# First-stage stores issued by ScalarE, split tiles doubled, rotation tables single

## The chip, the cores and the metric

The kernel runs on one core of one Trainium2 chip. The time is that of one execution on the device, in microseconds (us). TensorE (PE in the profile) multiplies, VectorE (DVE), ScalarE (ACT) and GpSimd (POOL) do elementwise work, and SyncE (SP) issues nearly all transfers. A transfer that SyncE, ScalarE or GpSimd issues runs on the core's 16 DMA engines. An engine takes its instructions in the order in which they stand in its queue, a transfer that it issues among them.

## The reference, cut to what matters

Two token groups (256 prompt tokens, 2048 noisy latent tokens) pass through two layers with the same weights. A layer normalises and modulates its input, projects it to 15 column groups, runs four mixers side by side and projects back:

```python
h = (rms_norm(x) * (1.0 + scale) + shift)
(da_q, da_k, da_v, da_g, s5_u, s5_g, hg_q, hg_ff, hg_fb, hg_i, hg_g,
 mla_cq, mla_ckv, mla_kr, mla_g) = split_columns(h @ P["w_in"][l])
q_r = rope_2d(q, *pos); k_all = concat([rope_2d(k, *pos), ck])   # differential attention
kr_lat = rope_2d(kr, *pos)                                       # latent attention
x = x + gate * (concat([a_out, b_out, c_out, d_out]) @ P["w_out"][l])
```

The outputs also hold the prompt's keys, values and final states of each layer. All is float32.

## The kernel before

A layer is run in three phases: `first_stage`, `mixers`, `out_proj`. Matmuls that need float32 accuracy are made of three: each operand is split by `split2` into a high part (a cast to fp32r, line 169, here on ScalarE) and a low part (the difference, line 173, here on VectorE), and `mm3` (lines 177 to 179) multiplies high by high, high by low and low by high.

`first_stage` weaves two generators. The one is `proj1`, in six blocks of 384 tokens. `prep` normalises the next block (`h_block`: transposing matmuls `pst` of line 299, scale and shift by ScalarE on line 304, high part `hhi` and low part `hlo` by VectorE) and `keep` stores both parts, 1.5 MB each, to `HD` (line 440). A block then has five column groups in the order dak0, dak1, daq0, daq1, cqk (keys, queries, and the rotated part of the latent keys with half of the compressed query): 24 matmuls each into a `psF` tile, followed by `evac1`; then three tiles `psT` of 24 matmuls, copied to `evT` (line 499) and stored to `VT` (line 500).

`evac1` is a chain through two engines. ScalarE copies the result from PSUM to `x32` (line 372 or 364, one buffer), VectorE turns it in four instructions with the tables `cos` and `sin` (`rope`, lines 324 to 328, one buffer), ScalarE casts the high part to `sphi` or `krhi` (one buffer under one tag), VectorE makes the low part `splo` or `krlo` (likewise), and SyncE stores: three transfers for keys and queries (`store_qk`, line 355), two for the rotated latent key (`store_kr`, lines 349 and 350). The buffer of a tile is free again when its last transfer has landed. In the last block, which holds the prompt, `out_tr` also transposes pieces of `x32` with matmuls `pso` (line 338) and stores them. `cache_keys` sends 256 cached keys down the same path at the start.

The other generator, `s5_build`, makes the tables of the state-space mixer: GpSimd and VectorE work out 16 groups (`wz`, `so`, `cp`, `Eb`), TensorE transposes and multiplies small tiles (`pswz`, `psk`, lines 1302 and 1307), ScalarE copies the results to `so` and `mp`, SyncE stores `SC` and `ED`.

PSUM in this stage: four buffers for `psF` and `psT` together (tag S), two for `pst` and `pso`, one each for two tags that `pswz` and `psk` share. A planner with a cost model orders the instructions of each engine when the program is built; the order is then fixed. The tables `cos` and `sin` come once per block by two transfers (`rope_tables`), and lie in a pool with two buffers. `rope_tables` and `out_tr` are also used in the next phase, there from a pool that has one buffer anyway.

Of the kernel before, what the change touches and what calls it, by code (L numbers as in the profile page):

```python
# [10 lines left out]
F32 = mybir.dt.float32  # L11
F32R = mybir.dt.float32r
# [12 lines left out]
LS = 2048  # L25
# [284 lines left out]
def rope_tables(g, p, tok0, n):  # L310
    nc = g.nc
    g.tab0 = tok0
    g.cos = p.tile([128, n], F32, tag="cos", name="cos")
    g.sin = p.tile([128, n], F32, tag="sin", name="sin")
    nc.sync.dma_start(g.cos, g.A["rcos"][:, tok0:tok0 + n])
    nc.sync.dma_start(g.sin, g.A["rsin"][:, tok0:tok0 + n])

# [14 lines left out]
def out_tr(g, p, src, rows, n, dst):  # L332
    nc = g.nc
    a, b = rows
    w = b - a
    for t in range(n // 128):
        ps = pst(g, "mm", "pso")
        nc.tensor.matmul(ps[:, :w], lhsT=src[a:b, t * 128:(t + 1) * 128], rhs=g.ident[a:b, a:b], start=True, stop=True)
        o = p.tile([128, 128], F32, tag="otr", name="otr")
        nc.scalar.copy(o[:, :w], ps[:, :w])  # L340
        nc.sync.dma_start(dst(t), o[:, :w])


def store_kr(g, p, src, tok0, n):
    nc = g.nc
    hi = p.tile([128, 384], F32R, tag="sphi", name="krhi", bufs=1)[64:96, :n]
    lo = p.tile([128, 384], F32R, tag="splo", name="krlo", bufs=1)[64:96, :n]
    split2(g, hi, lo, src)
    nc.sync.dma_start(g.KRD[0, 0:32, tok0:tok0 + n], hi.bitcast(F32))
    nc.sync.dma_start(g.KRD[1, 0:32, tok0:tok0 + n], lo.bitcast(F32))  # L350


def store_qk(g, dst, parts, idx, hi, lo, sl):
    for r, part in enumerate(parts):
        g.nc.sync.dma_start(dst[4 * idx:4 * idx + 4, r * 32:(r + 1) * 32, sl], (hi, lo)[part].bitcast(F32))


def evac1(g, l, p, kind, idx, ps, tok0, n):
    nc = g.nc
    sl = slice(tok0, tok0 + n)  # L360
    cut = min(max(LS - tok0, 0), n)
    x32 = p.tile([128, 384], F32, tag="x32", name="x32", bufs=1)
    if kind == "cqk":
        nc.scalar.copy(x32[:96], ps[:96, :n])
        r0 = FROW[(kind, idx)]
        nc.sync.dma_start(g.PF[r0:r0 + 64, sl], x32[:64])
        if cut < n:
            out_tr(g, p, x32[:, cut:], (64, 96), n - cut, lambda t: g.O["new_mla_krope"][l, t * 128:(t + 1) * 128, :])
        r32 = rope(g, p, x32, (64, 96), tok0, n, "rp")
        store_kr(g, p, r32[64:96], tok0, n)  # L370
        return
    nc.scalar.mul(x32, ps[:, :n], 32 ** -0.5 if kind == "daq" else 1.0)
    if kind == "dak" and cut < n:
        out_tr(g, p, x32[:, cut:], (0, 128), n - cut, lambda t: g.O["new_diff_k"][l, t * 128:(t + 1) * 128, idx * 128:(idx + 1) * 128])
    r32 = rope(g, p, x32, (0, 128), tok0, n, "rp")
    hi = p.tile([128, 384], F32R, tag="sphi", name="sphi", bufs=1)
    lo = p.tile([128, 384], F32R, tag="splo", name="splo", bufs=1)
    split2(g, hi, lo, r32)
    store_qk(g, g.QD if kind == "daq" else g.KD, (0, 0, 1) if kind == "daq" else (0, 1, 0), idx, hi, lo, sl)

# [25 lines left out]
def cache_keys(g, l, p):  # L406
    nc = g.nc
    for i in range(2):
        kc32 = p.tile([128, 384], F32, tag="x32", name="kc32", bufs=1)
        nc.sync.dma_start(kc32[:, :256], g.A["cdk"][l, i])  # L410
        hi = p.tile([128, 384], F32R, tag="sphi", name="sphi", bufs=1)
        lo = p.tile([128, 384], F32R, tag="splo", name="splo", bufs=1)
        split2(g, hi[:, :256], lo[:, :256], kc32[:, :256])
        store_qk(g, g.KD, (0, 1, 0), i, hi[:, :256], lo[:, :256], slice(NT, NK))
    kr32 = p.tile([128, 384], F32, tag="x32", name="kr32", bufs=1)[64:96, :256]
    nc.sync.dma_start(kr32, g.A["cmr"][l])
    store_kr(g, p, kr32, NT, 256)


def proj1(g, l):  # L420
    nc = g.nc
    N = 384
    with ExitStack() as es:
        px = es.enter_context(pool(g, "pjx", 2))
        ph0 = es.enter_context(pool(g, "pjh0", 1))
        pw0 = es.enter_context(pool(g, "pjw0", 1))
        pws = es.enter_context(pool(g, "pjs", 2))
        starts = list(range(0, NT, N))
        hs = {}

        def prep(i):
            ph = ph1 if i % 2 else ph0
            hi = ph.tile([128, 8, N], F32R, tag="hhi", name="hhi")
            lo = ph.tile([128, 8, N], F32R, tag="hlo", name="hlo")
            h_block(g, l, starts[i], N, px, hi, lo, mod if i == 0 else None)
            hs[i] = (hi, lo)

        def keep(i):
            for part, x in enumerate(hs[i]):
                nc.sync.dma_start(g.HD[part, :, :, starts[i]:starts[i] + N], x.bitcast(F32))  # L440

        mod = startup(g) if l == 0 else None
        pw = es.enter_context(pool(g, "pjw", 1))
        prep(0)
        ph1 = es.enter_context(pool(g, "pjh1", 1))
        p = es.enter_context(pool(g, "pj", 2))
        wf = []

        def load_f(k):
            m = len(FB1[k][2])  # L450
            w32 = pws.tile([128, 8, 128], F32, tag="w32", name="w32")
            q = pw0 if k == 0 else pw
            hi = q.tile([128, 8, 128], F32R, name=f"wfh{k}")
            lo = q.tile([128, 8, 128], F32R, name=f"wfl{k}")
            nc.sync.dma_start(w32[:, :, :m], g.A["wF"][l, k] if m == 128 else g.A["wFp"][l])
            split2(g, hi[:, :, :m], lo[:, :, :m], w32[:, :, :m], "act", "vec" if k == 0 else W1LO)
            wf.append((hi, lo))

        load_f(0)
        if l == 0:  # L460
            late_consts(g)
        for k in range(1, len(FB1)):
            load_f(k)
        wth = pw.tile([128, 8, 512], F32R, name="wth")
        wtl = pw.tile([128, 8, 512], F32R, name="wtl")
        for kc in range(0, 8, 2):
            w32 = pws.tile([128, 2, 512], F32, tag="w32", name="wt32")
            nc.sync.dma_start(w32, g.A["wT"][l, :, kc:kc + 2, :])
            split2(g, wth[:, kc:kc + 2, :], wtl[:, kc:kc + 2, :], w32, "act", W1LO)
        keep(0)  # L470
        yield
        cache_keys(g, l, p)
        for i, tok0 in enumerate(starts):
            if 0 < i < len(starts) - 1:
                prep(i + 1)
                keep(i + 1)
            if i == 2 and l == 0:
                for rows in [g.KRD[0, 32:34]] + [g.KD[i, 96:98] for i in range(8)]:
                    nc.sync.dma_start(rows.rearrange("o (a b) -> (o a) b", b=128), g.ones[0:2 * NK // 128, :])
            hi, lo = hs.pop(i)  # L480
            rope_tables(g, p, tok0, N)
            for k, (kind, idx, cols) in enumerate(FB1):
                if i == 0 and k == H1:
                    prep(1)
                    keep(1)
                m = len(cols)
                ps = pst(g, "mm", "psF")
                for kc in range(8):
                    mm3(nc, ps[:m, :N], wf[k][0][:, kc, :m], wf[k][1][:, kc, :m], hi[:, kc, :], lo[:, kc, :], kc == 0, kc == 7)
                evac1(g, l, p, kind, idx, ps, tok0, N)  # L490
                yield
            for t in range(N // 128):
                ts_ = slice(t * 128, (t + 1) * 128)
                tok = tok0 + t * 128
                ps = pst(g, "mm", "psT")
                for kc in range(8):
                    mm3(nc, ps, hi[:, kc, ts_], lo[:, kc, ts_], wth[:, kc, :], wtl[:, kc, :], kc == 0, kc == 7)
                o = p.tile([128, 512], F32, tag="ev", name="evT")
                nc.scalar.copy(o, ps)
                (nc.gpsimd if i + 1 == len(starts) else nc.sync).dma_start(g.VT[tok:tok + 128, :], o)  # L500
                if tok >= LS:
                    nc.sync.dma_start(g.O["new_diff_v"][l, tok - LS:tok - LS + 128, :], o[:, 0:256])
                yield


# [654 lines left out]
def s5_build(g, l, p1, pb):  # L1160
    nc = g.nc
# [18 lines left out]
    k, t = t16("k"), t16("t")  # L1180
# [85 lines left out]
    SC = g.SC[l]  # L1266
# [29 lines left out]
    def emit(gi, wz, so, cp, br_):  # L1296
# [3 lines left out]
        for i in range(2):  # L1300
            ps_ = pst(g, "mm", "pswz")
            nc.tensor.transpose(ps_[:, 0:128], wz[i].rearrange("p s c -> p c s").rearrange("p c s -> p (c s)"), g.ident)
            nc.scalar.copy(so[:, i, :], ps_[:, 0:128])
        nc.sync.dma_start(SC[gi, :, 0:4, :], so)
        psk = pst(g, "mm", "psk")
        for i in range(2):
            nc.tensor.matmul(psk[:, :240], lhsT=br_[i].rearrange("p s c -> p c s").rearrange("p c s -> p (c s)"), rhs=cp[i].rearrange("p t h -> p (t h)"), start=(i == 0), stop=(i == 1))
# [500 lines left out]
```

## Time and profile before

| | |
|---|---|
| median of 3 runs | 5360.32 us (5353.59 to 5371.05) |
| profiled execution | 5377.43 us, span 5375.6 us, mean granted clock 0.927 |
| busy over the span | TensorE 4758.3 us (89%), VectorE 3834.8 (71%), ScalarE 3178.6 (59%), GpSimd 1086.8 (20%) |
| moved by DMA | 599.37 MB, mean 111 GB/s |

The profile holds one execution. "Busy" counts instructions that compute; a matmul is counted with its pipeline, so that a busy TensorE may still run below its peak. A wait is put down to what released it. `x<-psF` means that tile `x` is made from tile `psF`; buffer numbers are left out of names, so `x32` is shown as `x`, and `sphi` stands for every tile of that name. SPq is the queue of SyncE.

### The profile page before, as it was taken

How to read it: one execution, taken by the hardware profiler on the slowest of the kernel's cores; microseconds unless marked ns; L12 is line 12 of the kernel's file. 1: busy time of each engine (PE TensorE's matmuls, PEld its weight loads, DVE VectorE, ACT ScalarE, POOL GpSimd, SP SyncE). 2: the span in 40 equal slices, each digit the busy share in tenths (PEclk: the TensorE clock that was granted, in tenths of full speed). 3: DMA queues.
4: the chain of work that ended last, by engine and by line, in shares of the span. 5: the costliest groups of instructions: out<-in, count | busy, mean ns of one | idle time of the engine just before them, and what ended most of it. 6: DMA issues, size and time to landing. Idle time of an engine off the chain costs nothing.

```text
span 5375.6 us, 81145 instructions
## 1 busy us (share of the span) xinstructions
PE 4758.3 (89%) x27920; PEld 3462.6 (64%) x27920; DVE 3834.8 (71%) x7616; ACT 3178.6 (59%) x7516; POOL 1086.8 (20%) x1323
## 2 busy tenths in 40 slices
PE   6787999999999997889978869999999989989999
PEld 5675767677666664446767747676776666644477
DVE  7654767676668886886677547676766678879877
ACT  3224877777777773235433257786777768743354
POOL 3751222222210000000227612222222100000022
PEclk8997999999998997999989979999999989989999
DMA  6455233443332214425445452334333321241253
GB/s 216 161 171 149 88 104 95 130 116 102 91 89 72 54 51 137 117 53 165 137 166 185 154 156 87 104 99 127 116 103 92 85 72 48 54 115 51 68 159 124
DMA packets 507523, 599.37 MB, mean 111 GB/s; under 512 B 147630, under 2 KB 414806, under 8 KB 507110
## 3 DMA queue, kind: packets, MB, share of 16 engines
q1 hardware_dynamic: 506630, 592.61, 36.9%
q8 instruction: 220, 3.60, 0.3%
q14 instruction: 193, 1.58, 0.1%
q0 software_dynamic: 480, 1.57, 0.1%
HBM read 378.42 MB, written 215.18 MB: 110 GB/s over the span
## 4 chain that ended last, share of the span: by engine, by line
PE 50%; DVE 18%; DMA 13%; ACT 10%; issue 4%; POOL 3%; SPq 2%; ACTq 0%; DVEq 0%; POOLq 0%
PE psav L858 5%; PE psS L870 4%; PE psF L177 4%; PE psF L178 4%; PE psF L179 4%; PE psS L817 4%; PE psmav L950 4%; ACT junk L820 3%; PE psM L961 3%; DVE nm L818 2%; DVE a L872 2%; DMA KD<-sphi 2%; ACT pp L871 2%; PE psM L963 2%; PE psM L962 2%
## 5 line engine op out<-in xcount | busy, mean ns | idle before, releaser
L818 DVE TENSOR_REDUCE nm<-psS 128x1 f32<-128x512 f32 (+1 forms) x1312 | 790.6, 626 | 353.5 <-PE psS L817 342.3
L820 ACT ACTIVATE junk<-psS,nm 128x512 bf16<-128x512 f32 (+1 forms) x1312 | 847.6, 646 | 205.9 <-DVE nm L818 186.8
L871 ACT ACTIVATE pp<-psS 128x512 f32<-128x512 f32 (+1 forms) x1184 | 653.2, 593 | 169.7 <-PE psS L870 164.0
L177 PE MATMUL psF<-h,whi 128*128 128x288 f32 x2304 | 701.7, 305 | 29.5 <-ACT whi L169 29.5
L872 DVE SCALAR_TENSOR_TENSOR a<-pp,nlam 128x512 f32<-128x512 f32 (+1 forms) x592 | 513.8, 870 | 258.4 <-ACT pp L871 257.4
L178 PE MATMUL psF<-h,whi 128*128 128x288 f32 x2304 | 692.0, 300 | 0.0
L179 PE MATMUL psF<-h,wlo 128*128 128x288 f32 x2304 | 689.4, 299 | 1.8 <-DVE wlo L173 1.8
L964 ACT ACTIVATE me<-psM 128x512 f32<-128x512 f32 (+1 forms) x592 | 345.4, 590 | 474.8 <-PE psM L963 436.4
L817 PE MATMUL psS<-ks,qs 96*128 96x512 f32 (+1 forms) x1312 | 544.0, 425 | 52.1 <-ACT junk L820 33.4
L870 PE MATMUL psS<-qs,ks 98*128 98x512 f32 (+1 forms) x1184 | 444.6, 440 | 54.8 <-ACT junk L820 39.5
L177 PEld LDWEIGHTS psF<-h,whi 128*128 128x128 f32 x2304 | 448.3, 195 | 62.6 <-ACT whi L169 31.2
L178 PEld LDWEIGHTS psF<-h,whi 128*128 128x128 f32 x2304 | 448.5, 195 | 55.6
L171 POOL CAST whi<-w 128x1024 fp32r<-128x1024 f32 x140 | 153.2, 1095 | 1626.1 <-PE psF L178 1302.9
L927 DVE TENSOR_REDUCE mnm<-psM 128x1 f32<-128x512 f32 (+1 forms) x656 | 393.3, 623 | 79.5 <-PE psM L926 77.4
L179 PEld LDWEIGHTS psF<-h,wlo 128*128 128x128 f32 x2304 | 445.5, 193 | 3.1 <-DVE wlo L173 3.1
L870 PEld LDWEIGHTS psS<-qs,ks 98*128 98x128 f32 x1184 | 206.3, 195 | 237.6 <-ACT junk L820 135.8
L817 PEld LDWEIGHTS psS<-ks,qs 96*128 96x128 f32 x1312 | 256.4, 198 | 156.7 <-ACT junk L820 93.3
L173 POOL TENSOR_TENSOR wlo<-w,whi 128x1024 fp32r<-128x1024 f32 x140 | 349.3, 2495 | 11.2
L967 DVE TENSOR_TENSOR macc<-macc,me 128x1024 f32<-128x1024 f32 x256 | 311.5, 1217 | 39.9 <-ACT me L964 38.4
L858 PE MATMUL psav<-a,dav 128*64 128x512 f32 (+1 forms) x1184 | 311.9, 647 | 17.0 <-DVE a L872 17.0
L961 PE MATMUL psM<-qs,ks 98*128 98x512 f32 (+1 forms) x592 | 274.3, 463 | 50.3 <-ACT me L964 23.6
L1369 POOL MEMSET s5rt<- 128x2 f32 x16 | 1.6, 101 | 1532.1 <-ACT s5rt L1368 1532.1
(451 smaller groups left out, 10525.5 us busy)
## 6 DMA issues: line engine op xcount, KB each, us to landing
w<-wF SPq DMA_DIRECT2D x152, 512.0 KB
h<-HD SPq DMA_DIRECT2D x64, 576.0 KB
wmod<-w_mod SPq DMA_DIRECT2D x48, 512.0 KB
HD<-hhi SPq DMA_DIRECT2D x12, 1536.0 KB
HD<-hlo SPq DMA_DIRECT2D x12, 1536.0 KB
GX<-ev SPq DMA_DIRECT2D x128, 144.0 KB
gt<-GX SPq DMA_DIRECT2D x36, 512.0 KB
PF<-ev SPq DMA_DIRECT2D x96, 144.0 KB
```

What stands on the lines that cost most here:

```text
L177: nc.tensor.matmul(out, lhsT=w_hi, rhs=x_hi, start=start, stop=False)
L178: nc.tensor.matmul(out, lhsT=w_hi, rhs=x_lo, start=False, stop=False)
L179: nc.tensor.matmul(out, lhsT=w_lo, rhs=x_hi, start=False, stop=stop)
L817: nc.tensor.matmul(ps[:, :kn], lhsT=qs[0:96, i, t * 128:(t + 1) * 128], rhs=key_cols(ks[i], k0, kn)[0:96], start=True, stop=True)
L818: nc.vector.tensor_reduce(nm[:, i, t, ci:ci + 1], ps[:, :kn], axis=AX.X, op=ALU.max, negate=True)
L820: nc.scalar.activation(out=junk[:, :kn], in_=ps[:, :kn], func=AF.Exp, bias=nm[:, i, t, ci:ci + 1], accum_out=sm[:, i, t, ci:ci + 1])
L858: x = nc.tensor.matmul(av[hh * 64:(hh + 1) * 64, :n], lhsT=v[:, kt, hh * 64:(hh + 1) * 64], rhs=aa[:, hh, :n], start=(ki == 0), stop=(ki = ...
L870: nc.tensor.matmul(ps[:, :n], lhsT=key_cols(ks[2 * hh + m], kt * 128, 128), rhs=qs[:, 2 * hh + m, :n], start=True, stop=True)
L871: nc.scalar.activation(out=pp[:, m, :n], in_=ps[:, :n], func=AF.Exp)
L872: last = nc.vector.scalar_tensor_tensor(aa[:, hh, :n], pp[:, 1, :n], nlam, pp[:, 0, :n], ALU.mult, ALU.add)
L927: nc.vector.tensor_reduce(nm[:, i, t, ci:ci + 1], ps[:, :kn], axis=AX.X, op=ALU.max, negate=True)
L961: nc.tensor.matmul(ps[:, :n], lhsT=kh, rhs=qq[:, i, :n], start=True, stop=False)
```

## The change

Fifteen lines change. Stores of tiles that ScalarE wrote last leave from ScalarE's queue: the high parts (`sphi`, `krhi`), `PF<-x`, `VT<-evT` and the copy of the values, the transposed outputs `otr`, and `SC<-so`. Low parts, `HD`, `ED` and the rest stay with SyncE. The tags `sphi` and `splo` get the pool's two buffers instead of one; `cos` and `sin` get one instead of two.

```diff
 def rope_tables(g, p, tok0, n):
-    g.cos = p.tile([128, n], F32, tag="cos", name="cos")
-    g.sin = p.tile([128, n], F32, tag="sin", name="sin")
+    g.cos = p.tile([128, n], F32, tag="cos", name="cos", bufs=1)
+    g.sin = p.tile([128, n], F32, tag="sin", name="sin", bufs=1)
...
         nc.scalar.copy(o[:, :w], ps[:, :w])
-        nc.sync.dma_start(dst(t), o[:, :w])
+        nc.scalar.dma_start(dst(t), o[:, :w])
...
 def store_kr(g, p, src, tok0, n):
-    hi = p.tile([128, 384], F32R, tag="sphi", name="krhi", bufs=1)[64:96, :n]
-    lo = p.tile([128, 384], F32R, tag="splo", name="krlo", bufs=1)[64:96, :n]
+    hi = p.tile([128, 384], F32R, tag="sphi", name="krhi")[64:96, :n]
+    lo = p.tile([128, 384], F32R, tag="splo", name="krlo")[64:96, :n]
     split2(g, hi, lo, src)
-    nc.sync.dma_start(g.KRD[0, 0:32, tok0:tok0 + n], hi.bitcast(F32))
+    nc.scalar.dma_start(g.KRD[0, 0:32, tok0:tok0 + n], hi.bitcast(F32))
     nc.sync.dma_start(g.KRD[1, 0:32, tok0:tok0 + n], lo.bitcast(F32))
 
 def store_qk(g, dst, parts, idx, hi, lo, sl):
     for r, part in enumerate(parts):
-        g.nc.sync.dma_start(dst[4 * idx:4 * idx + 4, r * 32:(r + 1) * 32, sl], (hi, lo)[part].bitcast(F32))
+        (g.nc.scalar, g.nc.sync)[part].dma_start(dst[4 * idx:4 * idx + 4, r * 32:(r + 1) * 32, sl], (hi, lo)[part].bitcast(F32))
...
-        nc.sync.dma_start(g.PF[r0:r0 + 64, sl], x32[:64])
+        nc.scalar.dma_start(g.PF[r0:r0 + 64, sl], x32[:64])
...
-    hi = p.tile([128, 384], F32R, tag="sphi", name="sphi", bufs=1)
-    lo = p.tile([128, 384], F32R, tag="splo", name="splo", bufs=1)
+    hi = p.tile([128, 384], F32R, tag="sphi", name="sphi")
+    lo = p.tile([128, 384], F32R, tag="splo", name="splo")
...
                 nc.scalar.copy(o, ps)
-                (nc.gpsimd if i + 1 == len(starts) else nc.sync).dma_start(g.VT[tok:tok + 128, :], o)
+                nc.scalar.dma_start(g.VT[tok:tok + 128, :], o)
                 if tok >= LS:
-                    nc.sync.dma_start(g.O["new_diff_v"][l, tok - LS:tok - LS + 128, :], o[:, 0:256])
+                    nc.scalar.dma_start(g.O["new_diff_v"][l, tok - LS:tok - LS + 128, :], o[:, 0:256])
...
-        nc.sync.dma_start(SC[gi, :, 0:4, :], so)
+        nc.scalar.dma_start(SC[gi, :, 0:4, :], so)
```

The two tiles in `cache_keys` change as those in `evac1` do.

## Rows read from the trace of the kernel before

**Rows 1.** Busy us (and instructions) by stretch: both first stages without their starts

```profile
core 0: us, PE busy (x) PEld busy (x) DVE busy (x) ACT busy (x) POOL busy (x), PEclk, DMA share, GB/s
114.00:460.00 346.00, 268.01 (x1321) 236.06 (x1319) 179.30 (x395) 80.29 (x185) 182.40 (x395) 0.91 0.47 149
2781.00:3133.00 352.00, 270.29 (x1348) 233.72 (x1347) 202.65 (x503) 89.19 (x201) 203.71 (x438) 0.89 0.50 159
```

**Rows 2.** Chain that ended last, 114 to 460 us: shares, then start us, us, what

```profile
by line: DMA QD<-splo 16.5%; DMA KD<-sphi 16.2%; DMA KD<-splo 10.6%; DMA SC<-so 4.3%; issue 3.0%; DVE splo L173 2.5%; POOL Eb L257 2.2%; POOL Eb L254 1.9%; SPq L355 1.8%; DMA QD<-sphi 1.8%; POOL t L256 1.8%; POOL Eb L255 1.7%; PE psT L178 1
...
430.11 6.54 DMA KD<-sphi
437.17 0.49 ACT x L372
437.85 6.10 DMA QD<-sphi
```

**Rows 3.** Waits of ScalarE, layer 0, 60 to 460 us: total us, times, longest

```profile
ACT sphi L169 <- DMA KD<-sphi: 71.8, 11, 10.7
ACT krhi L169 <- DMA QD<-sphi: 44.8, 6, 8.4
ACT sphi L169 <- DMA QD<-sphi: 34.9, 6, 11.8
```

**Rows 4.** Waits of ScalarE, layer 1, 2760 to 3133 us

```profile
ACT sphi L169 <- DMA KD<-sphi: 70.6, 8, 21.5
ACT krhi L169 <- DMA QD<-sphi: 34.5, 5, 8.9
...
ACT sphi L169 <- DMA QD<-sphi: 22.0, 5, 6.5
```

**Rows 5.** Waits of TensorE, layer 0, 60 to 460 us

```profile
PE psk L1307 <- DVE cp L254: 29.7, 7, 12.4
PE pswz L1302 <- ACT mp L1308: 17.2, 7, 4.8
...
PE pso L338 <- ACT x L364: 10.6, 1, 10.6
PE pso L338 <- ACT x L372: 9.2, 1, 9.2
```

**Rows 6.** Waits of TensorE, layer 1, 2760 to 3133 us

```profile
PE pso L338 <- ACT x L364: 23.1, 1, 23.1
PE psk L1307 <- DVE cp L254: 20.5, 9, 4.6
...
PE pst L299 <- ACT t L304: 9.7, 3, 6.1
PE psk L1307 <- DVE cp L257: 8.2, 5, 4.6
```

**Rows 7.** Timeline of ScalarE in layer 0's last block (idle before, releaser)

```profile
426.39 0.51 ACT L169 CAST sphi<-rt 128x384 fp32r<-128x384 f32 x1 [9.18 <-DMA KD<-sphi]
```

**Rows 8.** SyncE's issues on lines 355 and 1304: ns min/median/max, first and last

```profile
L355 SPq DMA_DIRECT2D KD<-sphi x56: 504/532/4230, 64.5 to 3106.9; - x56
L355 SPq DMA_DIRECT2D QD<-sphi x48: 510/518/2244, 129.3 to 3122.1; - x48
...
L1304 SPq DMA_DIRECT2D SC<-so x32: 319/373/3745, 110.5 to 3061.7; - x32
```

**Rows 9.** Timeline of TensorE after a wait in layer 0's last block

```profile
414.12 0.52 PE L177 MATMUL psF<-hhi,wfh 128*128 128x384 f32 x1
414.44 0.52 PE L178 MATMUL psF<-hlo,wfh 128*128 128x384 f32 x1
...
419.32 0.33 PE L177 MATMUL psF<-hhi,wfh 128*128 128x384 f32 x1
419.50 0.33 PE L178 MATMUL psF<-hlo,wfh 128*128 128x384 f32 x1
```

**Rows 10.** Chain that ended last, layer 1's first table load: start us, us, what

```profile
2737.59 3.20 DMA cos<-rcos
```

**Rows 11.** Waits of GpSimd, 0 to 460 us and 2700 to 3140 us

```profile
POOL VT L500 <- ACT evT L499: 78.6, 2, 77.6
...
POOL VT L500 <- ACT evT L499: 64.2, 3, 57.0
```

**Rows 12.** Timeline of SyncE's queue, layer 0's second block: start us, us

```profile
174.56 2.01 SPq L440 DMA_DIRECT2D HD<-hlo  x1
176.62 3.65 SPq L355 DMA_DIRECT2D KD<-sphi  x1
```

More of the change, by code (lines that the diff above doesn't have):

```diff
@@ L410, in cache_keys @@
         nc.sync.dma_start(kc32[:, :256], g.A["cdk"][l, i])
-        hi = p.tile([128, 384], F32R, tag="sphi", name="sphi", bufs=1)
-        lo = p.tile([128, 384], F32R, tag="splo", name="splo", bufs=1)
+        hi = p.tile([128, 384], F32R, tag="sphi", name="sphi")
+        lo = p.tile([128, 384], F32R, tag="splo", name="splo")
         split2(g, hi[:, :256], lo[:, :256], kc32[:, :256])
```

## The prediction

> **What bounds the kernel now.** The kernel is TensorE's over most of its span, but the change touches the two first stages alone, so I read those by stretch before anything else. In both, TensorE is idle: 346 - 268.0 = 78 us in layer 0 and 352 - 270.3 = 82 us in layer 1, at a granted clock of 0.91 and 0.89 [rows 1]. VectorE is at 52 and 58%, GpSimd at 53 and 58%, ScalarE at 23 and 25%: no engine fills the stage, so it is bound by a chain. The chain of waits says which: in layer 0 the stores of split tiles take 16.5 + 16.2 + 10.6 + 1.8 = 45% of it, and in the last block it is store, copy, store with hardly any arithmetic between [rows 2]. That is the one-buffer loop of `evac1`: a cast can't begin before the last store of the cast before has landed. The waits of ScalarE give it a size: the cast stood for landings 71.8 + 44.8 + 34.9 = 151.5 us in layer 0 [rows 3] and 70.6 + 34.5 + 22.0 = 127.1 us in layer 1 [rows 4]. ScalarE also empties TensorE's PSUM banks and serves the state-space tables, so everything queued behind the cast is late; VectorE stands behind it, since the low part needs the cast. What this costs is read from TensorE's own waits: `psk` for VectorE's `cp` (29.7 us; layer 1 20.5 + 8.2), `pswz` for ScalarE's `mp` (17.2), and the prompt's transposes `pso` for `x` (10.6 + 9.2; layer 1 23.1) [rows 5, 6].
>
> **The change part by part: the buffers.** With two buffers a cast waits for the store of the cast before the last. A step without the wait is the copy, four instructions of rope, the cast and the low part; in the last block the cast that ended a 9.18 us wait shows the size of what goes [rows 7]. One step takes about 0.5 + 2.3 + 0.5 + 0.5 us and some hops, and with two issues put into ScalarE's queue (below) I take 5.2 us. Five steps make 26 us, against 268 / 6 = 45 us of TensorE's work in a block [rows 1]: TensorE sets the pace again, and four PSUM buffers let it run ahead of the chain.
>
> I take back TensorE's waits by their releaser. Where VectorE or ScalarE was late because it stood at a split tile (`psk` for `cp`, `pswz` for `mp`), three quarters: GpSimd feeds the same chain and is late by itself at times. Layer 0: 0.75 x (29.7 + 17.2) = 35.2. Layer 1: 0.75 x 28.7 = 21.5. The `pso` waits are the chain of the last block running behind; they go, less two issues in each of five steps, 5 x 1.1 = 5.5 us: 19.8 - 5.5 = 14.3, and 23.1 - 5.5 = 17.6. `pst` for `t` in layer 1 is mixed; half, 4.9 [rows 5, 6]. Together 49.5 + 44.0 = 93.5 us. Below it the bound is nothing; above it all of TensorE's idle time, 78 + 82 = 160 us.
>
> **The clock.** After the wait that ends the last block's transposes the matmuls of `psF` follow each other at 0.32 us, some 5 us later at 0.18 [rows 9]: after a wait the granted clock is at the lower of its two levels, 1.2 of 2.4 GHz. With fewer waits less is run at that level. If the mean goes a third of the way to full, 0.91 to 0.94 and 0.89 to 0.93, the busy time shrinks by 268 x 0.03 / 0.94 = 8.6 and 270 x 0.04 / 0.93 = 11.6 us [rows 1]: 20 us; the bounds are 0 and 268 x 0.09 + 270 x 0.11 = 54 us.
>
> **Issues on ScalarE.** Each layer moves 109 issues: 28 `KD` and 24 `QD` high parts, 18 `VT`, 16 `SC`, 7 `KRD`, 6 `PF`, 10 outputs. An issue of line 355 took 532 and 518 ns in the median on SyncE, one of `SC` 373 [rows 8]. At 0.53 us for those that have no row here, that is 28 x 0.53 + 24 x 0.52 + 16 x 0.37 + 41 x 0.53 = 55 us per layer, so ScalarE's 80 to 89 us become some 140 of 346: room enough. The trace has no issue from ScalarE; SyncE's row is the nearest, with its ends 0.3 us and 4.23 us [rows 8]. Queued behind each issue are the next copy out of PSUM, the modulation `t` and the copies `so` and `mp`, and TensorE waits for these. What is on its path is the 5.5 us per last block, already taken off; the cover for the rest is the PSUM run-ahead, and without it all 55 us would count.
>
> **What SyncE loses, and the queues.** SyncE's low parts, `HD`, tables and loads no longer stand behind these 109 issues. A high part's store no longer stands behind them either: behind a 1.5 MB `HD` store its issue alone took 3.65 us [rows 12]. The last block's `VT` leaves GpSimd, which had stood 78.6 and 64.2 us at the end of the stage with nothing behind it [rows 11]: nothing gained. That time is also GpSimd's reserve: its 182 and 204 us of work fit into a stage 50 us shorter. Its links with `psk` and `pswz` will show up more; with an order of the planner that may place them worse I take off 12 us, bounds 0 and 40. Data on the way are the same bytes.
>
> **The rule on queues.** The Trainium skill, DMA: Bandwidth & Descriptors, section Issuing engines are not separate DMA queues, says that transfers started by any engine share the same 16 DMA engines, and that spreading them saves only the time of issuing. By it the landing stays as it is and only the buffers act, which is the second rival, at -58 us instead of -101; no row of before shows a store from ScalarE.
>
> **One rotation table.** The next block's tables now wait for the last rope of this one. A load took 3.20 us where the chain shows one [rows 10]; between that rope and the next lie 72 matmuls of `psT`, about 16 us on TensorE. I cost it at nothing; without that cover 10 loads x 3.2 = 32 us, and SyncE's queue stands as long.
>
> **Sum.** 93.5 + 20 - 12 = 101 us off the profiled execution: 5377.4 - 101 = 5276. It lies 17 us above the median of the runs, so I forecast 5360.3 - 101 = 5259 us.
>
> **The rivals.** *Slower: ScalarE is held by its own issues.* If issuing beside SyncE is dear, as the 3.65 us behind an `HD` store suggest [rows 12], ScalarE trades a wait for a wait. Now it stands 151.5 + 127.1 = 278.6 us for landings; over 218 issues that is 1.28 us, and a mean issue above this makes the stage longer. At 2 us ScalarE is held 157 us more; TensorE lost 160 us for those 278.6, so at that ratio 90 us: 5450. For it: nearly every step has an issue behind it. Against it: the median of 0.53 us [rows 8]. Beside it stands the Trainium skill, Perfetto Trace Analysis, section DMA Instruction — HWDGE (DVE, Sync): an issuing sequencer takes a lock on a shared descriptor generator first.
>
> *Landing as late as before.* If stores land no sooner, a wait beyond one step of 5.2 us stays. The mean waits were 6.5, 7.5 and 5.8 us in layer 0, and 8.8, 6.9 and 4.4 in layer 1 [rows 3, 4], so about 1.3 x 11 + 2.3 x 6 + 0.6 x 6 + 3.6 x 8 + 1.7 x 5 = 69 of 278.6 stay, a quarter. Then 0.75 x 93.5 - 12 = 58 us, without the clock: 5302.
>
> *TensorE without idle time.* All 160 us and 20 of clock: 5180. Against it: GpSimd's share of the waits.
>
> *No change.* The planner's new order, or a table load on the path (32 us) with GpSimd's bound of 40, eats most of the 93.5: within 16 us of 5360.
>
> **How the numbers follow.** The forecast (75 to 130 us off) 0.50; landing as late (20 to 75) 0.22; no idle time (beyond 130) 0.08; no change 0.08; slower 0.12. A difference of 0.3%, 16 us, is about what a measurement of this kernel can tell from none; so faster 0.80, same 0.08, slower 0.12. The range runs from 5190, which leaves some 0.04 beyond it, to 5345, with 0.16 to 0.18 above it. The forecast's own range is 5230 to 5285.
>
> **What would show it.** In the profile after: casts in the first stages no longer wait for landings (now 278.6 us), or under 70 us; issues on ScalarE's queue at about 0.5 us; the stages shorter by 40 to 60 us each, GpSimd ending nearer to their end; TensorE's clock there above 0.91. I am wrong if ScalarE's issues last above 1.3 us in the mean, if low parts queued on SyncE behind `HD` take over the wait of the high parts, if table loads end waits of rope, or if a later phase gives the time back.

## The result and the profile after

The changed kernel takes 5299.75 us (median of four executions, 5290.25 to 5308.8) against 5359.34 us of the kernel before: a ratio of 0.9886, 95% interval 0.9868 to 0.9904, so 60 us or 1.1% faster. The forecast was 5259 us. The direction and the whole range (5190 to 5345) held; 5299.75 lies above the forecast's own 5230 to 5285 us. Of 101 us forecast, 60 came. An execution that ran at a lower granted clock throughout (one of four in each of two experiments, in one of them the profiled one) is left out of every time, ratio and row here and below.

The profiled execution has a span of 5288.5 us, 87 us below that of before. The two first stages give 56 of it: the first `psF<-h,whi` of the next stage stands at 459.1 us instead of 486.9, and from layer 1's first load of `X` to its last `evT` it is 2669.1 to 3069.0 = 399.9 us instead of 2709.2 to 3137.4 = 428.2. The rest is mostly scatter, as far as the medians tell: before's execution was 18 us above its median, after's 10 below.

From mark to mark, columns as in [rows 1], first before (two rows), then after:

```profile
0.00:486.90 486.90, 355.44 (x1845) 299.05 (x1845) 276.31 (x786) 141.47 (x295) 221.77 (x460) 0.87 0.56 179
2709.20:3137.40 428.20, 328.10 (x1637) 284.74 (x1635) 256.35 (x726) 114.92 (x241) 224.14 (x454) 0.89 0.52 169
...
0.00:459.10 459.10, 350.75 (x1844) 295.19 (x1844) 276.05 (x786) 143.50 (x295) 224.80 (x457) 0.87 0.59 190
2669.10:3069.00 399.90, 323.14 (x1637) 282.54 (x1635) 256.99 (x726) 116.48 (x240) 226.06 (x452) 0.92 0.54 178
```

TensorE ran the same matmuls. Its busy time fell by 4.7 and 5.0 us; its idle time fell from 131.5 to 108.4 us in layer 0 and from 100.1 to 76.8 in layer 1. That is 10 us and 46 us, together the 56. The granted clock is 0.87 as before in layer 0, and 0.92 for 0.89 in layer 1.

TensorE's waits after, 114 to 430 us (us in total, times, longest):

```profile
PE psk L1307 <- ACT so L1303: 24.7, 5, 9.1
PE pswz L1302 <- POOL wz L257: 12.2, 6, 5.3
PE pso L338 <- ACT x L372: 5.5, 1, 5.5
PE pswz L1302 <- ACT mp L1308: 3.9, 2, 3.0
...
PE psk L1307 <- DVE cp L254: 1.7, 3, 0.7
```

And 2721 to 3070 us:

```profile
PE psk L1307 <- DVE cp L254: 11.0, 8, 2.3
PE pst L299 <- DVE dg L287: 9.6, 1, 9.6
PE pswz L1302 <- POOL wz L257: 9.0, 7, 3.3
PE pswz L1302 <- POOL Eb L252: 8.9, 1, 8.9
PE pst L299 <- DVE ph L1200: 6.1, 1, 6.1
PE pswz L1302 <- ACT mp L1308: 5.6, 1, 5.6
PE pswz L1302 <- ACT so L1303: 3.8, 1, 3.8
...
PE psk L1307 <- DVE cp L257: 1.7, 2, 1.3
```

Two things are to be seen against [rows 5, 6]. The first goes by what released a wait. The waits that the prediction named are nearly gone. In layer 0 `psk` for `cp`, `pswz` for `mp` and `pso` for `x` fell from 66.7 to 2.1 + 3.9 + 5.9 = 11.9 us. In layer 1 `psk` for `cp`, `pso` for `x` and `pst` for `t` fell from 61.5 to 12.7. That is 54.8 + 48.8 = 103.6 us back. But other waits stand in their place, first of all 24.7 us of `psk` behind ScalarE's copies `so`, a link that isn't in [rows 5], then GpSimd's `wz` and `Eb` and VectorE's `ph`. All rows of the view together went from 77.0 (114 to 460 us) to 52.4 us in layer 0, and from 95.6 (2760 to 3133 us) to 63.8 in layer 1: the net is 24.6 + 31.8 = 56.4 us. (The waits of this view are another measure than the idle time above, which fell by 46 us.) So 103.6 - 56.4 = 47.2 us came back as waits at the next links.

The second goes by what waited. Before, the view had these rows too, in layer 0 and then in layer 1:

```profile
PE pswz L1302 <- POOL wz L257: 6.5, 4, 3.2
...
PE pst L299 <- DVE dg L287: 13.1, 2, 12.9
...
PE pswz L1302 <- POOL wz L257: 7.6, 5, 2.7
```

All rows added up by the tile that waited, in us:

| | layer 0 before | after | layer 1 before | after |
|---|---|---|---|---|
| `psk` | 31.1 | 28.2 | 31.1 | 14.4 |
| `pswz` | 26.1 | 18.3 | 14.2 | 30.8 |
| `pso` | 19.8 | 5.9 | 23.1 | 0 |
| `pst` | 0 | 0 | 22.8 | 15.7 |
| `psF`, `psT` | 0 | 0 | 4.4 | 2.9 |

In layer 0 `psk` waits nearly as long as before, only for another: it needs a PSUM buffer as well as `cp`, and the copy `so`, which empties one, now comes last. In layer 1 `pswz` lost what `psk` got back. So the small matmuls of the state-space build together got back 10.7 + 0.1 us; what came back are the prompt's transposes `pso`, 13.9 + 23.1 = 37.0 us, and `pst`, 7.1 us.

Where `so` is late is shown by ScalarE's own waits for transfers, 114 to 430 us (seven of twenty rows):

```profile
ACT so L1303 <- DMA HD<-hlo: 25.6, 3, 11.9
...
ACT krhi L169 <- DMA QD<-sphi: 11.1, 3, 7.0
ACT evT L499 <- DMA KD<-splo: 9.2, 1, 9.2
ACT evT L499 <- DMA QD<-splo: 9.1, 1, 9.1
...
ACT sphi L169 <- DMA HD<-hhi: 8.3, 1, 8.3
ACT x L364 <- DMA QD<-sphi: 8.0, 1, 8.0
...
ACT sphi L169 <- DMA KD<-sphi: 3.8, 1, 3.8
```

The casts' waits for the stores of their own tiles, 151.5 us in [rows 3], are 11.1 + 3.8 = 14.9 us. Yet ScalarE's waits for transfers altogether fell only from 161.5 us (114 to 460 us) to 117.1. The copy `so` has nothing to do with `HD<-hlo`. One such place in ScalarE's timeline (ACTq rows are issues; in brackets the idle time before and its releaser):

```profile
167.56 0.51 ACT L169 CAST sphi<-rt 128x384 fp32r<-128x384 f32 x1 [2.79 <-DVE rt L328]
...
168.11 0.51 ACTq L355 DMA_DIRECT2D QD<-sphi  x1
168.66 0.36 ACT L1308 COPY mp<-psk 128x240 f32<-128x240 f32 x1 [0.19 <-ACT x L372]
177.01 0.53 ACTq L355 DMA_DIRECT2D QD<-sphi  x1
177.64 0.27 ACT L1303 COPY so<-pswz 128x128 f32<-128x128 f32 x1 [8.62 <-DMA HD<-hlo]
```

The tile's data is ready at 167.56 + 0.51 = 168.07 us, one store of it goes at once, the second 8.9 us after the first, and the copy behind it with it. The reason stands in the built program, in the waits of ScalarE's queue (the stores at 168.11 and 177.01 us are those of `sphi_1792`):

```
L355 DMA QD_76<-sphi_1001 4x32x384 [waits DMAHW1_49,Activation_49]
...
L355 DMA QD_76<-sphi_1792 4x32x384 [waits DMAHW1_49,Activation_49]
L355 DMA QD_76<-sphi_1792 4x32x384 [waits DMAHW3_49]
```

Transfers issued by SyncE and ScalarE take turns on eight completion semaphores, and one waits until the earlier transfer on its semaphore has landed, whoever issued that. The one before the second store of `sphi_1792`, on `DMAHW3_49`, is a 1.5 MB store that SyncE had issued at 159.72 us:

```profile
159.72 0.64 SPq L440 DMA_DIRECT2D HD<-hlo  x1
```

170 of the 218 transfers now in ScalarE's queue have such a wait at them or right before them. The Trainium skill, DMA: Bandwidth & Descriptors, section Why a DMA increments its semaphore by 16 and not by 1, says why a program does this: with two transfers in flight on one semaphore, part of the second can be counted for the first. On SyncE such a wait holds only other transfers; on ScalarE it holds what empties PSUM.

The issues themselves (ns min/median/max, first and last):

```profile
L355 ACTq DMA_DIRECT2D KD<-sphi x56: 512/527/1071, 60.5 to 3039.4; - x56
...
L1304 ACTq DMA_DIRECT2D SC<-so x32: 321/326/1147, 105.3 to 3017.4; - x32
```

They cost what SyncE's did in [rows 8], less in the worst case. (A row counts the issue, not the wait before it.)

### The profile page after: what moved, and what is told of

The parts are those of the page before. It is cut to its first block, busy times and chain, and to the rows that moved or that the text cites. A ratio compares the mean times of both kernels' runs of the same rounds, so it can differ in the third digit from the quotient of the medians.

```text
span 5288.5 us, 80997 instructions
## 1 busy us (share of the span) xinstructions
PE 4713.3 (89%) x27920; PEld 3438.2 (65%) x27920; DVE 3834.6 (73%) x7616; ACT 3182.6 (60%) x7516; POOL 1090.9 (21%) x1317
## 4 chain that ended last, share of the span: by engine, by line
PE 51%; DVE 17%; DMA 12%; ACT 11%; issue 4%; POOL 3%; SPq 1%; ACTq 0%; DVEq 0%; POOLq 0%
PE psav L858 5%; PE psF L177 4%; PE psS L870 4%; PE psF L178 4%; PE psF L179 4%; PE psmav L950 4%; PE psS L817 4%; ACT junk L820 3%; PE psM L961 2%; DVE nm L818 2%; DVE a L872 2%; ACT pp L871 2%; PE psM L926 2%; PE psM L962 2%; PE psM L963 2%
## 5 line engine op out<-in xcount | busy, mean ns | idle before, releaser
L950 PE MATMUL psmav<-me,mv 128*64 128x512 f32 (+1 forms) x1184 | 311.2, 625 | 16.3 <-ACT me L964 11.2
```

What stands on the lines that cost most here:

```text
L950: x = nc.tensor.matmul(av[i * 64:(i + 1) * 64, :n], lhsT=v[:, kts[ki], i * 64:(i + 1) * 64], rhs=e[:, i, :n], start=(ki == 0), stop=(ki == ...
```

## The experiments

Ratios are to the kernel before on the same chip, with the 95% interval. Stages are given as "layer 0's end / layer 1's length" by the two marks above: 486.9 / 428.2 us before, 459.1 / 399.9 us after.

**The buffers alone.** All stores are issued by their engines of before.

```diff
-        (g.nc.scalar, g.nc.sync)[part].dma_start(...)
+        g.nc.sync.dma_start(...)
...
-        nc.scalar.dma_start(SC[gi, :, 0:4, :], so)
+        nc.sync.dma_start(SC[gi, :, 0:4, :], so)
```

> The kernel before with two buffers for the split tiles and one for the rotation tables; every store leaves from the engine it left from before. The change came to 5299.8 us against 5359.3. In its trace both first stages together are 56 us shorter, and ScalarE's queue stands for landings of transfers that hold none of its data: 170 of the 218 transfers in its queue carry a wait on one of eight completion semaphores that SyncE's transfers use too. Theory A (the buffers give the gain, the move to ScalarE costs part of it): as fast as the change or faster, 5270 to 5305 us, and ScalarE's waits for landings below 60 us per layer. Rival B (the move gives the gain, since high parts no longer stand behind large stores in SyncE's queue): 5320 to 5350 us, with casts and low parts still waiting for landings of the store before the last.

Measured: 5301.95 us, 0.9881 [0.9853, 0.9909]; stages 466.5 / 398.8. The buffers by themselves give the whole gain, and no cost of the move is to be seen; Rival B falls. Its ScalarE waits, 60 to 480 us:

```profile
ACT sphi L169 <- DMA KD<-sphi: 48.8, 7, 13.0
...
ACT evT L499 <- DMA VT<-evT: 27.6, 4, 10.1
...
ACT krhi L169 <- DMA QD<-sphi: 21.1, 5, 7.5
```

These three alone are 97.5 us, so that part of Theory A, under 60 us, missed. The casts still wait 70 us in layer 0, unlike in the change (14.9), and the time is the same. For TensorE the small matmuls give little here too: from mark to mark `psk` and `pswz` wait 49.0 us in layer 0 and 36.4 in layer 1, against 59.0 and 45.3 before and 49.7 and 45.2 in the change.

**The queue alone.** Stores on ScalarE, one buffer for each split tile and two for the tables as before.

```diff
-    hi = p.tile([128, 384], F32R, tag="sphi", name="sphi")
+    hi = p.tile([128, 384], F32R, tag="sphi", name="sphi", bufs=1)
```

> The change with one buffer for the split tiles and two for the tables, as before; only the issuing engine of the stores is changed. Theory A (the buffers give the gain, the move costs): no gain or slower, 5350 to 5400 us, since a cast waits for its landing as before and ScalarE now stands for unrelated landings too. Rival B (the move gives the gain): 5300 to 5330 us, since a high part's store is issued right behind its cast and lands sooner.

Measured: 5356.45 us, 0.9979 [0.9965, 0.9994]; stages 493.2 / 417.8. Theory A held. Moving 218 issues is worth 0.2%, by its interval 0.35% at most. The casts' waits for their own tiles' stores in layer 0 are

```profile
ACT sphi L169 <- DMA KD<-sphi: 44.2, 8, 9.8
ACT krhi L169 <- DMA QD<-sphi: 43.8, 6, 9.6
...
ACT sphi L169 <- DMA QD<-sphi: 12.1, 2, 7.1
```

They are 100.1 us, for 151.5 before: the move by itself took a third of these waits, and the time hardly followed.

**The change with the `HD` stores given to GpSimd**, so that the longest transfers leave the eight semaphores.

```diff
-                nc.sync.dma_start(g.HD[part, ...], x.bitcast(F32))
+                nc.gpsimd.dma_start(g.HD[part, ...], x.bitcast(F32))
```

> The change with the 24 stores of HD (1.5 MB each) issued by GpSimd instead of SyncE: they then take no part in the eight completion semaphores that SyncE's and ScalarE's transfers share. Theory A (what holds ScalarE's queue are waits for unrelated landings, the long ones first): ScalarE's waits released by HD (33.9 us in layer 0 of the change) are gone, the first stages are shorter by 10 to 25 us each, 5255 to 5285 us. Rival C (ScalarE is held by its own data or by the number of transfers, whatever their length): 5290 to 5310 us as the change, the waits going to other transfers. GpSimd's issue of so many pieces may cost it some us each, which would show as waits for wz and tw.

Measured: 5307.5 us, 0.9884 [0.9851, 0.9917]; stages 458.6 / 423.1. The waits of `so` for `HD` are gone, and others came, as ScalarE's waits show, 60 to 460 us:

```profile
ACT krhi L169 <- DMA QD<-sphi: 35.1, 5, 15.7
...
ACT so L1303 <- DMA QD<-sphi: 12.2, 1, 12.2
```

That `HD` in the shared semaphores keeps the missing 40 us is not borne out: layer 0's stage is as long as in the change. In layer 1 it is 23 us longer, and GpSimd's issues cost something there, as the expectation feared. TensorE's wait for the `wz` of line 254, 3.5 us in the change, is now, 2690 to 3112 us,

```profile
PE pswz L1302 <- POOL wz L254: 14.9, 6, 5.5
```

so that this run alone can't rule out a small gain behind it.

**The change with only the high parts on ScalarE** (118 transfers; `VT`, `SC`, `PF` and outputs as before).

```diff
-        nc.scalar.dma_start(SC[gi, :, 0:4, :], so)
+        nc.sync.dma_start(SC[gi, :, 0:4, :], so)
```

> The change with only the high parts (sphi, krhi) issued by ScalarE: 118 transfers instead of 218; VT, SC, PF and the transposed outputs leave from SyncE (the last block's VT from GpSimd) as before. Theory A (each transfer in ScalarE's queue is a chance to stand for an unrelated landing): faster than the change by 10 to 25 us, 5275 to 5290. Rival B (the move gives the gain): slower than the change by 5 to 20 us.

Measured: 5328.13 us, 0.9931 [0.9909, 0.9953]; stages 467.0 / 402.1. In the ratio's terms it is 24 us slower than the change, whose interval ends at 0.9904, and 27 us slower than the buffers alone. Theory A falls. It is slower, as Rival B said, by a little more, but not for its reason: the two runs before show that the move doesn't give the gain.

**One rotation table alone**, in the kernel before.

```diff
-    g.cos = p.tile([128, n], F32, tag="cos", name="cos")
+    g.cos = p.tile([128, n], F32, tag="cos", name="cos", bufs=1)
```

> The kernel before with one buffer for each rotation table instead of two and nothing else. Theory A (the load is hidden behind the 72 matmuls of psT): within 0.3% of before. Rival E (ten loads per run end waits of rope, 3 to 7 us each): 0.4 to 1.3% slower.

Measured: 5355.53 us, 0.9984 [0.9973, 0.9995]. The tables cost nothing; Rival E falls.

**The other half of the move**: high parts back on SyncE; `VT`, `SC`, `PF` and outputs on ScalarE.

```diff
-        (g.nc.scalar, g.nc.sync)[part].dma_start(...)
+        g.nc.sync.dma_start(...)
```

> The change with the high parts (sphi, krhi) back on SyncE: ScalarE issues VT, SC, PF and the outputs only; two buffers for the split tiles. Measured so far as a ratio to before: buffers only 0.9881, buffers and high parts on ScalarE 0.9931, the whole change 0.9886. Theory D (the parts of the move add up: the high parts on ScalarE cost 0.5%, the others give 0.45%): 0.982 to 0.985. Rival F (the move gives nothing either way, and these differences come from the order that the planner makes of each variant): 0.986 to 0.992.

Measured: 5312.56 us, 0.9905 [0.9889, 0.9922]. That can't be told from the change or from the buffers alone; Theory D falls, Rival F's range held. The two halves don't add up: with the high parts alone the move costs half of a per cent, with the rest added nothing. In the built programs each of these kernels has another order of instructions on its engines. That the order makes these differences is likely, but not shown: no run changed a part and kept the order.

**Without the small matmuls of the state-space build**, once in the kernel before and once in the change. The transposes `pswz` and the products `psk` are left out and ScalarE copies constants in their place.

```diff
-            nc.tensor.transpose(ps_[:, 0:128], wz[i]..., g.ident)
-            nc.scalar.copy(so[:, i, :], ps_[:, 0:128])
+            nc.scalar.copy(so[:, i, :], g.ident)
```

> The kernel before without the 64 small matmuls and transposes per layer of the state-space tables (pswz, psk): ScalarE copies a constant into so and mp instead, so the state-space branch computes something else; all else stays. It is the base for the next kernel. Theory G (TensorE's time before was lost to split tiles that stood for landings, the small matmuls only showed it): the matmuls' own work goes, some 30 us per layer of TensorE, but the stage stays bound by the stores: faster than before by 0 to 30 us in all. Rival H (the small matmuls bound the stage already): faster by 60 us or more.

> The change without the same small matmuls (a constant in their place, as in the kernel before it in this set). Theory G (with the buffers doubled, TensorE now waits for the state-space tables instead, 57 of its 93 us of waits in layer 0 of the change): the change is worth more here than the 59 us that it gave in the whole kernel, 85 to 130 us against the kernel before without the matmuls. Rival H (the rest is lost to ScalarE's queue or elsewhere): again 50 to 70 us.

Measured: 5337.02 us, 0.9945 [0.9924, 0.9966], and 5288.26 us, 0.9838 [0.9807, 0.987]; stages 472.0 / 406.6 and 460.3 / 389.4. Leaving the small matmuls out gives the kernel before 25 us, which is Theory G's. The change is worth 48.8 us there (57 us by the ratios), which is about Rival H's, and not the 85 and more that it would be if TensorE lost the rest at these matmuls. It is also nearly the 60 us of the whole kernel: for the most part the gain of the change doesn't come by way of the small matmuls, as the table above says too. TensorE then waits elsewhere; its largest wait in layer 0 of the changed kernel without them is

```profile
PE pst L299 <- ACT t L304: 56.7, 9, 17.1
```

the transposes of the `h` blocks, which stand behind ScalarE's modulation `t`. In the kernel of before without them it is 60.7 us.

**Fewer transfers, in three ways.** The next theory was that eight transfers in flight pace the whole stage. First, the eight small stores of each `mp` tile, which place its bands, become one plain store, 28 transfers fewer per layer of some 206:

```diff
-            for s in range(8):
-                nc.sync.dma_start(SC[g4:g4 + 4, s:128:8, 4, :]..., mp[s:128:8, :, ...])
+            nc.sync.dma_start(SC[g4:g4 + 4, :, 4, :]..., mp[:, :, 0:128])
```

> The change, with the eight small stores of each mp tile made into one of the whole tile (so the banded part of SC is wrong; 28 transfers fewer per layer, of some 206 that the first layer's first stage issues to the eight shared completion semaphores; the same bytes four times over, all else as in the change). Theory L (the stage is now paced by eight transfers in flight, each waiting for the one before it on its semaphore, so fewer transfers end it sooner): 28 of 206 is 14% of them; 10 to 20 us less in each first stage, 5255 to 5282 us. Rival R (the number of transfers doesn't pace it; what is left are the casts' own chain through rope and the small matmuls' operands): 5290 to 5310 us, within 0.3% of the change.

Measured: 5297.96 us, 0.9877 [0.9854, 0.9899]; stages 460.8 / 401.3. Second, the stores of `Eb` and `mp` are issued by GpSimd (`E.dma_start` for `nc.sync.dma_start`), in the change and then in the kernel of the buffers alone:

> The change, with the stores of Eb and mp (16 and 32 in each first stage) issued by GpSimd instead of SyncE, so that they leave the eight shared semaphores. Theory L: 48 of 206 transfers fewer in the ring, the long ones of Eb among them: 10 to 25 us less in each first stage, 5245 to 5280 us. Rival R: GpSimd issued a store in 0.85 us where the HD stores were given to it, 48 of them are 41 us of GpSimd per layer in a build that TensorE waits for at pswz: 0 to 15 us more per stage, 5300 to 5330 us.

> The kernel before with the change of buffers alone (5302 us) and the stores of Eb and mp issued by GpSimd. Here no compute stands behind a store in its queue, the casts wait for the landing of the tile before last. Theory L: landings come sooner with 48 transfers fewer in the ring, the casts' 107 us of waits per layer fall to 60 to 80, 5260 to 5290 us. Rival R: as with the change, 5300 to 5330 us.

Measured: 5297.18 us, 0.9878 [0.9854, 0.9902], stages 459.2 / 397.4; and 5309.01 us, 0.9901 [0.9878, 0.9923], stages 463.7 / 405.4. None differs from the change or from the buffers alone by what can be told apart. Taking 28 or 48 transfers off the semaphores doesn't shorten the stage; Theory L falls. TensorE's largest wait in layer 0 (60 to 460 us) is nearly that of the change in the first of the two kernels, and another in the second:

```profile
PE psk L1307 <- ACT so L1303: 23.5, 4, 7.3
...
PE pswz L1302 <- POOL wz L257: 20.2, 5, 7.4
```

In the second, where ScalarE issues nothing, `psk` stands 0.8 us for `so`; with the buffers alone, where it issues nothing either, 4.0. The waits of 12 us and more for `so` are all in kernels with these stores in ScalarE's queue, though not in each of them: with the `HD` stores on GpSimd it is 7.1. Without them GpSimd's `wz` takes more.

**The ceiling of the buffers.** Stores of split tiles take a constant tile, so that no cast waits for a landing; the casts are still made.

```diff
-        g.nc.sync.dma_start(dst[...], (hi, lo)[part].bitcast(F32))
+        g.nc.sync.dma_start(dst[...], g.zt[:, :hi.shape[1]])
```

> The kernel of the buffers alone, but the stores of the split tiles take their data from one constant tile, so no cast ever waits for the landing of a store of its tile (one buffer for each half is then enough; rope, casts and the number and size of the stores are as before, all issued by SyncE; keys and queries are constants, which the later stages read). It is the ceiling of what the buffers can take back. Theory C (the casts' waits for landings, 107 us in the first layer of the buffers-only kernel, still reach TensorE): each first stage 15 to 30 us shorter than with the buffers alone (466.5 and 399 us there), 440 to 450 and 370 to 385 us. Theory D (two buffers took back all that these waits cost TensorE; what is left comes of the state-space build and the h blocks): stages of 458 to 470 and 392 to 402 us. The stages decide, since constant data may change the later ones. Total 5240 to 5270 us by C, 5285 to 5310 us by D.

Measured: 5368.31 us, 1.0011 [0.9996, 1.0025]; stages 496.0 / 432.7. Both theories missed: with no cast waiting for a landing the kernel is as slow as before. The issues of these stores:

```profile
L355 SPq DMA_DIRECT2D KD<-zt x84: 503/1198/4457, 56.5 to 2912.6; - x84
L355 SPq DMA_DIRECT2D QD<-zt x72: 507/1862/4097, 92.8 to 2924.5; - x72
```

With no producer to wait for, the stores were ordered far ahead of the others and went out in bursts. Its chain of waits shows SyncE held from 112 to 156 us (start us, us, what):

```profile
by line: SPq L355 16.0%; DMA SC<-so 5.4%; PE psF L179 5.4%; PE psF L178 5.3%; PE psF L177 5.3%; DMA QD<-zt 3.2%; PE psT L177 2.9%; PE psT L178 2.8%; PE psT L179 2.8%; issue 2.8%; DMA xt<-x_s 2.8%; DMA sin<-rsin 2.6%; POOL Eb L254 2.4%; POOL
...
116.88 1.86 SPq L355
118.79 1.86 SPq L355
```

What stands behind in SyncE's order lands late, and its tiles come free late; ScalarE's waits, 60 to 500 us:

```profile
ACT evT L501 <- DMA VT<-evT: 39.7, 2, 30.6
```

and TensorE's, behind these:

```profile
PE psk L1309 <- ACT so L1305: 21.8, 1, 21.8
PE psF L177 <- ACT x L372: 21.3, 1, 21.3
```

So this is no clean ceiling: it removes the casts' waits and adds a jam on SyncE. It shows how a landing wait taken from one tile comes back at another tile of the same queue.

## Why the prediction was right or wrong, point by point

**What bounds the stages: right, and shown.** The one-buffer loop cost the 60 us: two buffers without the move give 0.9881, all of it, and the move without them 0.9979. Of TensorE's 160 us of idle time in [rows 1] it was the smaller part.

**TensorE's waits taken back, 93.5 us: the sum came, the mechanism only in part.** By the releaser's name 103.6 us went: `cp` and `mp` 40.9 of 46.9 us in layer 0 (35.2 taken) and `cp` 16.0 of 28.7 in layer 1 (21.5 taken), `pso` 13.9 and 23.1 (14.3 and 17.6), `pst` for `t` 9.7 (4.9). The `pso` terms are right, and `pso` is where the gain lies. The other large term, three quarters of `psk` and `pswz`, 56.7 us, is where the prediction went astray. It took the releaser of a wait for the only thing that was late. These matmuls have several operands and a PSUM buffer to wait for, and the next of them was nearly as late: together they got back 10.8 us.

**SyncE, the queues and the order: the same error, in the term that was to cover it.** "Its links with `psk` and `pswz` will show up more; with an order of the planner that may place them worse I take off 12 us, bounds 0 and 40." It measured 47.2 us, beyond its bound. It named GpSimd's links, and these did come (`wz` from 8.9 to 14.4 us in layer 0, `Eb` 8.9 in layer 1), but the largest, 24.7 us, is ScalarE's `so` behind a transfer in ScalarE's queue that waits for another to land. The prediction counted the moved issues and left out the waits that each issue carries. That mechanism is shown in the timeline; that it costs the 40 us isn't, for the buffers alone have none of it and are as fast.

**The clock, 20 us: mis-sized.** It measured 10 us, by TensorE's busy time over both stages. In layer 0 the granted clock stayed, and the rise from 0.91 to 0.94 that was forecast there didn't come. In layer 1 it rose about as forecast, from 0.89 to 0.92, but the busy time fell by 5.0 us and not by 11.6. By the releasers' names the sum in measured terms is 103.6 + 10 - 47.2 = 66 us; by idle and busy time it is 46 + 10 = 56 us, and the runs have 60.

**Its signs.** The stages were to be 40 to 60 us shorter each, and were 28. The casts' waits for their own stores, to be under 70 us, were 14.9 + 6.9.

**Issues on ScalarE: right.** 0.527 us in the median for line 355 (0.53 taken), 0.33 for `SC`. The slower rival needed 1.28 us in the mean and is out; the 218 issues on record have 0.54. Its idea, that ScalarE trades a wait for a wait, came true by the way of the semaphores. Of the lock that the Trainium skill names (Perfetto Trace Analysis, section DMA Instruction — HWDGE (DVE, Sync)) these medians show nothing.

**One rotation table, 0 us: right**, by the run with it alone. In the change one wait of rope for `cos` is left in layer 0, 2.8 us.

**The rule on queues.** By the Trainium skill, DMA: Bandwidth & Descriptors, section Issuing engines are not separate DMA queues, spreading issues saves only the time of issuing, so only the buffers would act. The runs agree: 0.9881 for the buffers alone, 0.9979 for the queue alone and 0.9886 for both.

**The rival "landing as late as before" had the number, -58 us, but not for its reason.** It expected 69 us of the casts' waits to stay in both layers. In the change 14.9 + 6.9 us stay for their own high parts; in the kernel of the buffers alone 69.9 us stay in layer 0 and 38.1 in layer 1, and the time is the same. So it was luck that its number came; how long casts wait no longer decides.

**What stays open** is which link holds the remaining 40 us. Taking `HD` off the shared semaphores, taking 28 or 48 transfers off them, and taking the small matmuls away each removed a wait that the trace had named, and each time the stages stayed about as long or grew, with other waits in their place. The runs fit several chains of nearly equal length through ScalarE, VectorE and GpSimd, in an order that the planner makes anew for each kernel; no run removed two of these links at once, so this is argued and not shown. The change with two table buffers was not tried, for want of room in SBUF. No version that does the whole work beat the change beyond its interval.

## What to carry to other kernels

When a loop's wait is removed, the waits that the trace names for it do go, but look at what else each waiting instruction needs, and price the link that is next: here 47 of 104 us went there. Add the waits up by what waited, too: 24.7 us of `psk` had only changed their name. A store issued by an engine that computes brings its waits along, for landings that have nothing to do with it; count those in the built program's queue, not only the time of the issues. And of a change with two parts, run each alone before explaining the sum: the move of 218 stores, the larger part of the diff, was worth 0.2%, and the second buffer of two tags the rest.

## What was not expected of the hardware

- A store of 192 KB that follows others of its kind without a gap took SyncE 1.86 us to issue instead of 0.51: 192 KB in 1.86 us is some 106 GB/s. The mean busy share of the 16 DMA engines is low meanwhile (last three columns: granted clock, share, GB/s), in the run with the constant tile and in the kernel before while it stores `QD`:

```profile
116.00:128.00 12.00, 12.00 (x61) 10.33 (x60) 10.83 (x25) 4.66 (x10) 10.53 (x24) 0.91 0.27 100
...
440.00:445.00 5.00, 0.01 (x1) 0.01 (x1) 0.00 (x0) 0.88 (x2) 0.00 (x0) 0.50 0.26 99
```

A mean hides what happens: 0.27 of 16 is 4.3. In the traces' packets four are under way at a time for 70% of the first stretch and 78% of the second, five for most of the rest, and never fewer than four. With large stores on the way (the change, 160 to 165 us, 400 GB/s) it is 16 to 19. So such a store seems to keep four engines busy throughout and to leave twelve idle. This bears on the loop itself, for the second stretch is the landing of `QD` that a cast waits for at the end of [rows 2]. The destination's outermost dimension in `store_qk` is 4; that this sets the number is likely, but no run here stores these tiles otherwise.
- GpSimd's issue of a 1.5 MB `HD` store took 0.86 to 0.90 us of its own time. SyncE's in the kernel before took 0.57 us for `hhi`, and 2.46 us in the median for `hlo`, which follows it at once:

```profile
L440 POOL DMA_DIRECT2D HD<-hlo x12: 847/902/943, 68.3 to 3021.7; - x12
...
L440 SPq DMA_DIRECT2D HD<-hlo x12: 549/2460/3942, 71.7 to 3043.3; - x12
```
